# Small fp32 matmuls split over tiles of 64 or 32 columns, and a later place for two operand sets and the FFN's weight buffers

## The chip, the cores and the metric

The program runs on one core of a Trainium2 chip. The metric is the device time of one execution in microseconds (us), as the median of several executions. TensorE has two clock levels, 1.2 and 2.4 GHz; the profile prints the granted clock as a share of the higher one.

## The reference

One inference step of a decoder layer: 512 new tokens of one prompt and one token each of 8 samples share the weights, so there are 520 token columns of 2048 channels. The part that matters here:

```
h = rms_norm(x, norm1); proj = h @ w_in                 # 2048 x 9232
DeltaNet, 8 heads of 128: conv, silu, l2norm(q), l2norm(k), chunks of 64 tokens (prompt)
    one token of a sample:  S' = S*exp(g); v' = (v - k.S')*beta; S'' = S' + k v'; o = q.S''
S5, 64 groups of 16 channels and 64 complex states: a scan along the tokens, y = Re(C x)
m = sigmoid(gate_d) * (o @ w_br_dn) + sigmoid(gate_s) * (glu(y) @ w_br_s5)
x = x + m @ w_out
h = rms_norm(x, norm2)
x = x + (silu(h @ w_ffn_gate) * (h @ w_ffn_up)) @ w_ffn_down   # hidden 5632
y = rms_norm(x, norm_f)
```

## The kernel before

**Large products.** Every fp32 weight matrix is read in blocks of 8 x 128 x 128 (`raw`), split by ScalarE (`whi`) and VectorE (`wlo`) into a rounded and a remainder part, and multiplied in three passes of fp32r with 260 moving columns (L94). From the FFN on the product is a Strassen scheme (L1367): seven products per pair of two blocks, on sums and differences of weight quarters (`s`, `sm`, `se`) and on seven prepared operand sets, B11, B21, T1, T2, T3, T4 and B22, each itself split into two parts in an SBUF slot (`put`).

**Small fp32 matmuls.** These have plain fp32 operands; the trace shows each as two records of a weight load and two of a matmul. Four places matter. In each of eight S5 batches `tables(bt)` makes `pkd` (a 128 x 32 stationary operand, 128 moving columns, eight matmuls in four column blocks of one PSUM tile, then one ScalarE copy `kd` and sixteen DMAs into the table `T_`), and `outputs(bt)` makes `py` from `T_` and the tokens and from `WR` and the scanned states `X` (16 matmuls with a 128 x 128 stationary operand and 72 moving columns). Each DeltaNet head makes `pss`, the sums of squares of its keys and queries (8 matmuls, 1 moving column), after GpSimd has squared them into `sq`. The sample states make `psk`, one matmul per sample and head (64 matmuls, 2 moving columns). Another S5 product, `pb` at L634, stands on 64-column tiles already before the change: its matmuls alternate between columns 0 to 63 and 64 to 127 of the array.

**Order.** The program is written as generators that yield between parts; a scheduler places instructions on each engine's queue by their dependencies and priorities, and the queues run in that order. The S5 batches, the heads and the sample states stand among the matmuls of large products, so that TensorE has work while they wait.

**The step into the FFN.** `add_squares` sums the squares of the residual rows into `ssq`; `rstd` sums over partitions with five small matmuls (`pr`), and GpSimd and VectorE make `rt` and `ms` from it, which `rows` spreads over all partitions with matmuls against the identity (`prb`). T4 and B22 are split in 16 parts by ScalarE and VectorE before the first FFN stream begins. The gate's first four `raw` blocks are SyncE DMAs at L1410. In the Strassen scheme the product z needs block A12 and the product "11" needs A11; T2 and T1 need the sum of A21 and A22, which GpSimd makes (L1346).

Of the kernel before, what the change touches and what calls it, by code (L numbers as in the profile page):

```python
# [33 lines left out]
def hybrid_step_kernel(  # L34
# [37 lines left out]
    def weights(src, k0, nk, col):  # L72
        raw = wp.tile([P, 8, P], F32, tag="raw", name="raw", bufs=3)
        hi = wp.tile([P, 8, P], F32R, tag="whi", name="whi")
        lo = wp.tile([P, 8, P], F32R, tag="wlo", name="wlo")
        nc.sync.dma_start(
# [434 lines left out]
    def s5_steps(upp):  # L511

        with ExitStack() as es:
# [31 lines left out]
            def tables(bt):  # L545
# [130 lines left out]
            def outputs(bt):  # L676
# [59 lines left out]
    def decode(dec, dd, de, ohi, olo):  # L736
# [82 lines left out]
    def dn_steps(ohi, olo):  # L819


        with ExitStack() as es:
# [83 lines left out]
            def prep(h):  # L906
# [299 lines left out]
    def squares(pool, at=None):  # L1206
# [11 lines left out]
        def rstd(pr=None, by=None):  # L1218

            if pr is None:  # L1220
                pr = pmt("pr")
            for c in range(4):
                PE.matmul(pr[:, c:c + 1], ssq[:, c * P:(c + 1) * P], ones[:, 0:1], start=True, stop=True)
            PE.matmul(pr[0:NB, 4:5], ssq[:, NTOK:T], ones[:, 0:1], start=True, stop=True)
# [27 lines left out]
    def put(name, q, src, scale=None):  # L1252

        hi, lo = parts(XS[name], q)
        if scale is None:
            A.activation(hi, src, AF.Copy)
# [7 lines left out]
    with tc.tile_pool(name="mp", bufs=8) as mp, tc.tile_pool(name="mq", bufs=2) as mq:  # L1264
        add_squares, rstd = squares(mq)
# [59 lines left out]
        rt, ms = rstd()  # L1325
# [82 lines left out]
    def block(src, k0, nk, col):  # L1408
        raw = wq.tile([P, 8, P], F32, tag="raw", name="raw", bufs=7)
# [8 lines left out]
    wp_s.close()  # L1418
    ww = ctx.enter_context(tc.tile_pool(name="ww", bufs=5, side="right"))
# [3 lines left out]
    wq_s = ctx.enter_context(ExitStack())  # L1423
    wq = wq_s.enter_context(tc.tile_pool(name="wq", bufs=4, side="right"))
# [6 lines left out]
    XS["T4"] = slot("xT4")  # L1431
    for q in range(8):
        b = acc(q)
        put("T4", q, b[:, 0:HF])
    b22 = [fp.tile([P, 4, HF], F32, tag="hu", name="b22") for _ in range(2)]
    for j in range(2):
        A.activation(b22[j], acc_[0][:, 4 * j:4 * j + 4, HF:T], AF.Copy)
    XS["B22"] = slot("xB22")
    for q in range(8):
        put("B22", q, b22[q // 4][:, q % 4])  # L1440
    sgate = [None]
    first = [True]

    def rows(dst, v):
        prb = [pmt("prb0"), pmt("prb1")]
        for c in range(4):
            PE.matmul(prb[0][:, c * P:(c + 1) * P], v[:, c:c + 1].to_broadcast([P, P]), ident, start=True, stop=True)
# [315 lines left out]
```

## Time and profile before

| | us |
|---|---|
| median of 3 executions | 2973.57 (2972.07 to 2979.77) |
| the profiled execution | 2972.03, span 2970.3 |
| mean granted clock of TensorE | 0.98 of full speed |
| 0 to 100 | norm, first projections |
| 100 to 430 | eight S5 batches among projections |
| 430 to 1050 | eight DeltaNet heads among projections |
| 1095 to 1230 | sample states among the products of w_glu |
| 1230 to 1570 | products of w_br and w_out |
| 1570 to 1610 | step into the FFN |
| 1610 to 2480, 2480 to 2960 | FFN gate and up, FFN down |

The stages are read from the lines at which TensorE works; all times in the rows count from the span's start. A row of the timeline that shows x2 for a small fp32 matmul is one instruction, because each has two records.

### The profile page before, as it was taken

To read this page: it belongs to the slowest core of one execution; us is meant where nothing else is said; L and a number is where in the kernel's file an instruction comes from. 1 tells how busy PE (TensorE), PEld (TensorE's weight loads), DVE (VectorE), ACT (ScalarE), POOL (GpSimd) and SP (SyncE) were. 2 spreads that over 40 slices of the span, in tenths; PEclk is the share of its full clock that TensorE was granted. 3 is DMA by queue.
4 is the path that set the end of the run, shared out by engine and by line. 5 is a ranking of instruction groups with operands and counts; after the bars stand their busy time and mean duration, and the time that the engine had idled before them with its cause. 6 is when DMAs were issued, how large, how long until landed. Compare 5 with 4: busy or idle time off the path is not lost.

```text
span 2970.3 us, 60986 instructions
## 1 busy us (share of the span) xinstructions
PE 2879.3 (97%) x23869; PEld 2844.5 (96%) x23869; DVE 2055.2 (69%) x3406; ACT 1279.2 (43%) x2229; POOL 1137.2 (38%) x1656
## 2 busy tenths in 40 slices
PE   8999999999999999999998999999999999999997
PEld 7999999889999999999998999999999998999997
DVE  5766444444455334643467999999999988999997
ACT  5244333223333222222254555555555555455555
POOL 0673402554444300310143555545555543222233
PEclk9999999999999998999998999999999999999999
DMA  6444443322333354844444555555555448755542
GB/s 165 109 126 124 126 129 100 79 70 71 78 79 77 100 145 142 247 143 118 125 126 128 154 158 167 162 173 167 159 160 168 154 151 303 250 196 181 182 135 87
DMA packets 640806, 424.23 MB, mean 143 GB/s; under 512 B 66550, under 2 KB 589783, under 8 KB 636887
## 3 DMA queue, kind: packets, MB, share of 16 engines
q1 hardware_dynamic: 640518, 420.34, 47.8%
q8 instruction: 188, 3.08, 0.4%
q14 instruction: 100, 0.81, 0.1%
HBM read 342.85 MB, written 75.18 MB: 141 GB/s over the span
## 4 chain that ended last, share of the span: by engine, by line
PE 77%; POOL 9%; DVE 6%; DMA 4%; issue 3%; ACT 1%; SPq 1%; POOLq 0%; ACTq 0%; DVEq 0%
PE pt L94 30%; PE px L1367 23%; PE py L1367 12%; PE pz L1367 6%; POOL tm L963 3%; POOL uu L965 2%; DVE wlo L70 2%; DMA dx<-xdsc 2%; PE psk L768 1%; PE pss L914 1%; DVE ac L1639 1%; POOL et L604 1%; POOL et L605 0%; DVE sm L1356 0%; PE pkq L944 0%
## 5 line engine op out<-in xcount | busy, mean ns | idle before, releaser
L70 DVE TENSOR_TENSOR wlo<-raw,whi 128x512 fp32r<-128x512 f32 (+1 forms) x485 | 527.0, 1101 | 244.7 <-ACT whi L78 194.4
L78 ACT ACTIVATE whi<-raw 128x1024 fp32r<-128x1024 f32 x218 | 231.0, 1060 | 638.6 <-PE pt L94 587.6
L94 PE MATMUL pt<-hhi,wlo 128*128 128x260 f32 (+1 forms) x2336 | 493.4, 289 | 4.1 <-DVE wlo L70 4.1
L94 PE MATMUL pt<-hlo,whi 128*128 128x260 f32 (+1 forms) x2336 | 493.6, 289 | 0.0
L94 PE MATMUL pt<-hhi,whi 128*128 128x260 f32 (+1 forms) x2336 | 490.9, 289 | 1.4 <-ACT pre L876 1.3
L94 PEld LDWEIGHTS pt<-hhi,wlo 128*128 128x128 f32 x2336 | 369.9, 192 | 7.2 <-DVE wlo L70 5.0
L94 PEld LDWEIGHTS pt<-hhi,whi 128*128 128x128 f32 x2336 | 368.5, 192 | 4.0 <-ACT pre L876 1.8
L94 PEld LDWEIGHTS pt<-hlo,whi 128*128 128x128 f32 x2336 | 370.4, 191 | 1.6 <-issue 0.2
L70 DVE TENSOR_TENSOR wlo<-s,whi 128x512 fp32r<-128x512 f32 (+1 forms) x272 | 319.5, 1188 | 3.8 <-ACT whi L1362 0.7
L1346 POOL TENSOR_TENSOR s<-raw 128x1024 f32<-128x1024 f32 (+1 forms) x90 | 216.9, 2411 | 255.1 <-DVE wlo L70 126.4
L1367 PE MATMUL px<-xT,whi 128*128 128x260 f32 x1408 | 257.6, 283 | 1.1 <-ACT u L1514 1.1
L1362 ACT ACTIVATE whi<-s 128x512 fp32r<-128x512 f32 (+1 forms) x272 | 167.8, 620 | 182.3 <-PE px L1367 100.3
L1362 ACT ACTIVATE whi<-raw 128x512 fp32r<-128x512 f32 (+1 forms) x267 | 166.4, 630 | 130.3 <-PE px L1367 71.0
L1367 PEld LDWEIGHTS px<-xT,whi 128*128 128x128 f32 x1408 | 217.3, 188 | 1.3 <-ACT u L1514 1.3
L1367 PE MATMUL px<-xT,wlo 128*128 128x260 f32 x704 | 199.2, 283 | 0.0
L1367 PE MATMUL px<-wx,whi 128*128 128x260 f32 x832 | 155.2, 284 | 3.4 <-ACT whi L1362 1.5
L1346 POOL TENSOR_TENSOR s<-raws 128x512 f32<-128x512 f32 (+1 forms) x64 | 79.7, 1248 | 193.5 <-DVE wlo L70 192.2
L1367 PE MATMUL pz<-xB,whi 128*128 128x260 f32 x704 | 133.2, 287 | 2.3 <-ACT whi L1362 2.3
L1367 PEld LDWEIGHTS px<-xT,wlo 128*128 128x128 f32 x704 | 132.5, 188 | 0.0
L1367 PEld LDWEIGHTS px<-wx,whi 128*128 128x128 f32 x832 | 127.5, 189 | 5.2 <-ACT whi L1362 2.1
L1367 PE MATMUL px<-xB,whi 128*128 128x260 f32 x704 | 129.5, 284 | 0.2 <-ACT whi L1362 0.2
L1367 PE MATMUL px<-xt,whi 128*128 128x260 f32 x704 | 129.3, 284 | 0.0
(586 smaller groups left out, 7611.6 us busy)
## 6 DMA issues: line engine op xcount, KB each, us to landing
raw<-in_w_in_dram SPq DMA_DIRECT2D x146, 512.0 KB
raw<-in_w_ffn_gate_dram SPq DMA_DIRECT2D x88, 512.0 KB
raw<-in_w_ffn_up_dram SPq DMA_DIRECT2D x88, 512.0 KB
xT<-hx SPq DMA_DIRECT2D x88, 260.0 KB
raws<-in_w_ffn_down_dram SPq DMA_DIRECT2D x44, 512.0 KB
xB<-hx SPq DMA_DIRECT2D x66, 260.0 KB
raw<-in_w_out_dram SPq DMA_DIRECT2D x32, 512.0 KB
hs<-xT SPq DMA_DIRECT2D x12, 1040.0 KB
```

The source lines that it names most:

```text
L70: V.tensor_tensor(out, full, hi.bitcast(F32), ALU.subtract)
L78: A.activation(hi[:, :nk], raw[:, :nk], AF.Copy)
L94: PE.matmul(pt[:, h, 0:c1 - c0], w_[:, j], x[:, c0:c1], start=k == 0 and i == 0, stop=k == n - 1 and i == 2)
L604: G.tensor_tensor(t1[:, r, :, 0:n], E[:, r, :, 0:n], rr, ALU.mult)
L768: PE.matmul(psk[:, 2 * i:2 * i + 2], sts[b][:, h], kqn[:, :, i], start=True, stop=True)
L914: PE.matmul(pss[:, s * 4 + c:s * 4 + c + 1], sq[:, s, c * P:(c + 1) * P], ones[:, 0:1], start=True, stop=True)
L963: G.tensor_tensor(tm[:, :, 0:31 - j], uu[:, :, j:j + 1].to_broadcast(sh), dx[:, j, j + 1:32].unsqueeze(1).to_broadcast(sh), ALU.mult)
L965: G.tensor_tensor(uu[:, :, j + 1:32], uu[:, :, j + 1:32], tm[:, :, 0:31 - j], ALU.add)
L1346: G.tensor_tensor(t, a, b, op)
L1362: A.activation(hi, w_in_, AF.Copy)
L1367: PE.matmul(o, w_[:, q - q0], x_, start=start and q == 0 and i == 0, stop=q == kp - 1 and i == 2, skip_group_check=not start)
L1639: V.tensor_tensor(a[:, j], o, a[:, j], ALU.add)
```

## The change

Six edits. `pkd` writes its four blocks to four column groups of 32 (positions 0, 32, 64, 96 of the array) with the two passes outermost, and `kd` is copied by four instructions of 32 x 128. `py`, `psk` and `pss` split each stationary operand of 128 columns into two of 64, on column groups 0 and 64: 128 to 256 matmuls for `py`, 64 to 128 each for `psk` and `pss`. `rstd` runs inside the first FFN stream, between its products, with `rows` after the third and fifth. T4 and B22 are split in four groups, behind products three to six, and pinned in that order. The FFN's `raw` blocks get a pool of their own (7 buffers) in the space that the projections' weights leave; A12 is loaded ahead of A11. In the FFN's down part all weight blocks come from that pool, and ten instead of eight halves of the operands lie in slots, four instead of six in the pool `hs`.

```diff
+                for r in range(2):
+                    for g in range(GB):
+                        PE.matmul(pkd[g * 32:(g + 1) * 32, 0:P], bd[:, r, g].rearrange("p a c -> p (a c)"),
+                                  W[:, r, g, 0:8].rearrange("p d c -> p (d c)"), start=r == 0, stop=r == 1,
+                                  tile_position=(0, g * 32))
+                kd = s1.tile([32, GB, P], F32, name="kd")
                 for g in range(GB):
-                    for r in range(2):
-                        PE.matmul(pkd[0:32, g * P:(g + 1) * P], bd[:, r, g].rearrange("p a c -> p (a c)"),
-                                  W[:, r, g, 0:8].rearrange("p d c -> p (d c)"), start=r == 0, stop=r == 1)
-                kd = s1.tile([32, GB, P], F32, name="kd")
-                A.activation(kd, pkd[0:32].rearrange("p (g m) -> p g m", g=GB), AF.Copy)
+                    A.activation(kd[:, g], pkd[g * 32:(g + 1) * 32, 0:P], AF.Copy)
...
+                        ms_ = [slice(m, m + 64) for m in range(0, P, 64)]
                         o = py[:, g * 72:(g + 1) * 72]
-                        PE.matmul(o, T_[:, g * 2 + g2], U_[:, g * 2 + g2, 0:72], start=True, stop=False)
-                        PE.matmul(o, WR[:, g, g2], X[:, g, g2, 0:72], start=False, stop=True)
+                        for m in ms_:
+                            PE.matmul(o[m], T_[:, g * 2 + g2, m], U_[:, g * 2 + g2, 0:72], start=True, stop=False)
+                        for m in ms_:
+                            PE.matmul(o[m], WR[:, g, g2, m], X[:, g, g2, 0:72], start=False, stop=True)
...
-                PE.matmul(psk[:, 2 * i:2 * i + 2], sts[b][:, h], kqn[:, :, i], start=True, stop=True)
+                for m in range(0, P, 64):
+                    PE.matmul(psk[m:m + 64, 2 * i:2 * i + 2], sts[b][:, h, m:m + 64], kqn[:, :, i],
+                              start=True, stop=True)
...
-                        PE.matmul(pss[:, s * 4 + c:s * 4 + c + 1], sq[:, s, c * P:(c + 1) * P], ones[:, 0:1],
-                                  start=True, stop=True)
+                        for m in range(0, P, 64):
+                            PE.matmul(pss[m:m + 64, s * 4 + c:s * 4 + c + 1], sq[:, s, c * P + m:c * P + m + 64],
+                                      ones[:, 0:1], start=True, stop=True)
...
-        rt, ms = rstd()
...
+    wq = ctx.enter_context(tc.tile_pool(name="wq", bufs=7, side="right"))
...
-        A_ = [[block(src, 8 * j, 8, (2 * i + n) * P) for j in range(2)] for n in range(2)]
+        A_ = [[block(src, 8 * j, 8, (2 * i + n) * P) for j in (1, 0)][::-1] for n in range(2)]
...
-            rows(rstd2, rt)
-            todo.append(lambda: rows(rms2, ms))
+            v = rstd(pinned=True)
+            rt.append(v[0])
+            sets = last_sets()
+            todo.extend([lambda: (rows(rstd2, v[0], "e"), sets[0]()), sets[1],
+                         lambda: (rows(rms2, v[1], "m"), sets[2]()), sets[3]])
...
-            hs_.append(ctx.enter_context(tc.tile_pool(name="hs", bufs=6)))
+            hs_.append(ctx.enter_context(tc.tile_pool(name="hs", bufs=4)))
...
-            if i < 8:
+            if i < 10:
                 return wx[i // 2][:, i % 2 * HW:(i % 2 + 1) * HW].rearrange("p (a b c) -> p a b c", a=4, b=2)
...
-                if first:
-                    raw = wq.tile([P, 8, P], F32, tag="raw", name="raw", bufs=7)[:, 0:2 * kp]
-                else:
-                    r = nth("raw", 6 if hs_ else 4)
-                    if r < 4:
-                        raw = raw_c[:, r * 1024:r * 1024 + 2 * kp * P].rearrange("p (k m) -> p k m", m=P)
-                    else:
-                        raw = hs_[1].tile([P, 8, P], F32, tag="rawx", name="rawx", bufs=2)[:, 0:2 * kp]
+                raw = wq.tile([P, 8, P], F32, name="raw")[:, 0:2 * kp]
```

The new function `last_sets` returns the four groups: four `put` of T4 and one ScalarE copy of a half of B22's source in each of the first two, four `put` of B22 in each of the others.

Three places of the order. First TensorE's queue at the sample states, before (L768 is `psk`, L94 the products of w_glu around it):

```order
L94 MATMUL pt<-g5hi,wlo 128x260 x2
L768 MATMUL psk<-kqn,st 128x2 x4
L94 MATMUL pt<-g5hi,whi 128x260 x2
L94 MATMUL pt<-g5lo,whi 128x260 x2
L768 MATMUL psk<-kqn,st 128x2 x2
...
L768 MATMUL psk<-kqn,st 128x2 x26
...
L768 MATMUL psk<-kqn,st 128x2 x32
```

And after (L774 is `psk`):

```order
L94 MATMUL pt<-g5hi,wlo 128x260 x2
L774 MATMUL psk<-kqn,st 64x2 x5
L94 MATMUL pt<-g5hi,whi 128x260 x2
L94 MATMUL pt<-g5lo,whi 128x260 x2
L774 MATMUL psk<-kqn,st 64x2 x3
...
L774 MATMUL psk<-kqn,st 64x2 x56
...
L774 MATMUL psk<-kqn,st 64x2 x64
```

The four runs of `psk` stay where they were, with the same matmuls of the large products between them; each has about twice the instructions, on operands half as wide.

Second TensorE's queue at the end of w_out (L94) and the begin of the first FFN stream, before (`pr` is `rstd`'s sum, `prb` is `rows`, `pz` and `px` are the products z and "11"):

```order
L94 MATMUL pt<-mhi,wlo 128x260 x2
L1223 MATMUL pr<-ones,ssq 128x1 x4
L1224 MATMUL pr<-ones,ssq 8x1
L1447 MATMUL prb_18549<-ident,rt 128x128 x4
L1448 MATMUL prb_18550<-ident,rt 128x8
L1367 MATMUL pz<-xB_17259,whi 128x260 x2
```

And after (L1375 is the Strassen product, `rstd_14990` the tile that now holds the sums of squares; between the first z row and `pr` stand the rest of z and of "11"):

```order
L94 MATMUL pt<-mhi,wlo 128x260 x2
L1375 MATMUL pz<-xB_17538,whi 128x260 x2
...
L1375 MATMUL px<-xB_17537,wlo 128x260
L1232 MATMUL pr<-ones,rstd_14990 128x1 x4
L1233 MATMUL pr<-ones,rstd_14990 8x1
L1375 MATMUL px<-xT_17539,whi 128x260 x2
```

The products z and "11" follow w_out's last matmul at once; `pr` stands behind them, `prb` later still.

Third SyncE's queue of DMAs at the same place, before (`asc` is the store of a residual row):

```order
L1302 DMA asc_14724<-acc_14703 128x520
L1302 DMA asc_14725<-acc_14703 128x520
L1302 DMA asc_14726<-acc_14703 128x520
L1410 DMA raw<-in_w_ffn_gate_dram 128x8x128 x4
L1410 DMA raw<-in_w_ffn_up_dram 128x8x128 x4
```

And after:

```order
L1311 DMA asc_15004<-acc_14983 128x520
L1311 DMA asc_15005<-acc_14983 128x520
L1418 DMA raw<-in_w_ffn_gate_dram 128x8x128 x2
L1311 DMA asc_15006<-acc_14983 128x520
L1418 DMA raw<-in_w_ffn_gate_dram 128x8x128 x2
L1418 DMA raw<-in_w_ffn_up_dram 128x8x128 x4
```

The gate's first two blocks, now A12 and A11, stand ahead of the last store. The first of them waits for w_out's last matmul (its buffer's former reader); before, it waited for `pr` and for VectorE's last split of w_out's rows.

## Rows read from the trace of the kernel before

**Rows 1.** The page, part 4: the chain that ended last, shares by engine.

```profile
PE 77%; POOL 9%; DVE 6%; DMA 4%; issue 3%; ACT 1%; SPq 1%; POOLq 0%; ACTq 0%; DVEq 0%
```

**Rows 2.** Stretches: length, busy us (xcount) of PE, PEld, DVE, ACT, POOL; PEclk, DMA share, GB/s.

```profile
100.00:227.00 127.00, 124.52 (x1101) 121.80 (x1099) 83.37 (x201) 49.36 (x72) 98.29 (x268) 1.00 0.46 117
227.00:430.00 203.00, 200.91 (x1780) 197.86 (x1781) 106.62 (x221) 79.90 (x112) 66.79 (x189) 1.00 0.48 128
1155.00:1190.00 35.00, 35.00 (x223) 35.00 (x222) 15.76 (x23) 5.37 (x8) 0.00 (x0) 0.71 0.18 58
1230.00:1570.00 340.00, 340.00 (x2843) 340.00 (x2842) 170.52 (x183) 109.70 (x156) 61.06 (x60) 1.00 0.45 132
1610.00:2310.00 700.00, 699.85 (x5828) 699.50 (x5828) 644.25 (x881) 382.22 (x726) 371.04 (x258) 1.00 0.53 161
```

**Rows 3.** Timeline, PE, first S5 batch: start us, us, line, operation, xcount.

```profile
127.07 1.93 PE L583 MATMUL pkd<-W,bd 128*32 128x128 f32 x16
...
128.93 1.22 PE L634 MATMUL pb<-uz,QT 128*64 128x72 f32 x32
...
130.08 0.51 PE L94 MATMUL pt<-hhi,wlo 128*128 128x260 f32 x2
...
130.43 0.40 PE L94 MATMUL pt<-hhi,whi 128*128 128x260 f32 x2
```

**Rows 4.** Timeline, PE, `py` of the fourth S5 batch, first and last L688 row.

```profile
259.39 0.44 PE L688 MATMUL py<-X,WR 128*128 128x72 f32 x2 [0.97 <-DVE X L665]
...
261.90 0.28 PE L688 MATMUL py<-X,WR 128*128 128x72 f32 x1
```

**Rows 5.** Waits of PE in 227 to 430: us in total, times, longest.

```profile
PE py L688 <- DVE X L665: 1.0, 1, 1.0
```

**Rows 6.** Timeline, PE, `pss` of one head.

```profile
797.23 0.38 PE L914 MATMUL pss<-ones,sq 128*128 128x1 f32 x2 [1.96 <-POOL sq L910]
...
798.00 1.70 PE L914 MATMUL pss<-ones,sq 128*128 128x1 f32 x14
799.56 0.78 PE L933 MATMUL pgc<-triu,gg 128*128 128x128 f32 x2
```

**Rows 7.** Timeline, PE, the two long runs of `psk` and what follows each.

```profile
1155.01 8.53 PE L768 MATMUL psk<-kqn,st 128*128 128x2 f32 x52
1163.40 0.78 PE L94 MATMUL pt<-g5hi,whi 128*128 128x260 f32 x2
...
1171.31 10.39 PE L768 MATMUL psk<-kqn,st 128*128 128x2 f32 x64
1181.57 0.78 PE L94 MATMUL pt<-g5hi,whi 128*128 128x260 f32 x2
...
1189.02 0.33 PE L783 MATMUL pq<-qk,ones 128*128 128x64 f32 x2
```

**Rows 8.** Timeline, 1570 to 1600: PE, then DVE, POOL and SyncE's queue.

```profile
1573.15 1.05 PE L1223 MATMUL pr<-ones,ssq 128*128 128x1 f32 x8 [2.75 <-DVE ssq L1216]
...
1576.44 2.07 PE L1447 MATMUL prb<-ident,rt 128*128 128x128 f32 x8 [2.11 <-POOL rt L117]
...
1581.33 0.80 PE L1367 MATMUL pz<-xB,whi 128*128 128x260 f32 x2 [2.29 <-ACT whi L1362]
...
1591.86 1.13 PE L1447 MATMUL prb<-ident,ms 128*128 128x128 f32 x8 [1.23 <-DVE se L1356]
...
1593.28 0.51 PE L1367 MATMUL py<-xT,whi 128*128 128x260 f32 x2
...
1579.64 2.46 DVE L70 TENSOR_TENSOR xB<-b,xB 128x260 fp32r<-128x260 f32 x7
...
1584.50 4.70 POOL L1346 TENSOR_TENSOR s<-raw 128x1024 f32<-128x1024 f32 x2 [8.11 <-DMA raw<-in_w_ffn_gate_dram]
...
1574.64 3.79 SPq L1410 DMA_DIRECT2D raw<-in_w_ffn_gate_dram  x4
```

**Rows 9.** DMA view, 1574 to 1590: rate in 40 slices of 0.4 us.

```profile
GB/s 0 0 0 0 79 159 301 315 343 342 314 297 293 251 262 294 292 321 315 302 294 288 291 292 291 291 289 289 292 292 289 288 293 288 289 234 99 6 0 0
```

More of the change, by code (lines that the diff above doesn't have):

```diff
@@ L1216, in add, with rstd @@
                 (V if t >= KD - 2 else G).tensor_tensor(ssq[:, h], ssq[:, h], sqt[:, h], ALU.add)
-        def rstd(pr=None, by=None):
+        def rstd(pr=None, by=None, pinned=False):
             if pr is None:
                 pr = pmt("pr")
+            pin = tc.keep_in_program_order if pinned else lambda m: m
             for c in range(4):
-                PE.matmul(pr[:, c:c + 1], ssq[:, c * P:(c + 1) * P], ones[:, 0:1], start=True, stop=True)
-            PE.matmul(pr[0:NB, 4:5], ssq[:, NTOK:T], ones[:, 0:1], start=True, stop=True)
+                pin(PE.matmul(pr[:, c:c + 1], ssq[:, c * P:(c + 1) * P], ones[:, 0:1], start=True, stop=True))
+            pin(PE.matmul(pr[0:NB, 4:5], ssq[:, NTOK:T], ones[:, 0:1], start=True, stop=True))
             rt, ms = (cp.tile([P, 5], F32, name=n) for n in (("rt", "ms") if by is None else ("rtf", "msf")))
@@ L1422, in hybrid_step_kernel @@
     rms2 = sp.tile([P, T], F32, name="rms2", bufs=1)
-    wq_s = ctx.enter_context(ExitStack())
-    wq = wq_s.enter_context(tc.tile_pool(name="wq", bufs=4, side="right"))
     def wparts(n):
@@ L1430, in hybrid_step_kernel, with last_sets, t4, b22_ @@
     fp = fp_s.enter_context(tc.tile_pool(name="fp", bufs=2))
[L1431 to L1441, printed above, removed]
-    first = [True]
-    def rows(dst, v):
-        prb = [pmt("prb0"), pmt("prb1")]
+    sgate, rt = [None], []
+    first = [True]
+    def last_sets():
+        pin = tc.keep_in_program_order
+        b22 = []
+        def t4(q0):
+            if not q0:
+                XS["T4"] = slot("xT4")
+            for q in range(q0, q0 + 4):
+                put("T4", q, acc(q)[:, 0:HF], pin=pin)
+            b22.append(fp.tile([P, 4, HF], F32, tag="hu", name="b22"))
+            pin(A.activation(b22[-1], acc_[0][:, q0:q0 + 4, HF:T], AF.Copy))
+        def b22_(q0):
+            if not q0:
+                XS["B22"] = slot("xB22")
+            for q in range(q0, q0 + 4):
+                put("B22", q, b22[q0 // 4][:, q - q0], pin=pin)
+        return [lambda: t4(0), lambda: t4(4), lambda: b22_(0), lambda: b22_(4)]
+    def rows(dst, v, tag):
+        prb = [pmt("prb0", tag), pmt("prb1", tag)]
+        pin = tc.keep_in_program_order
         for c in range(4):
-            PE.matmul(prb[0][:, c * P:(c + 1) * P], v[:, c:c + 1].to_broadcast([P, P]), ident, start=True, stop=True)
-        PE.matmul(prb[1][:, 0:NB], v[0:NB, 4:5].to_broadcast([NB, P]), ident[0:NB, 0:NB], start=True, stop=True)
+            pin(PE.matmul(prb[0][:, c * P:(c + 1) * P], v[:, c:c + 1].to_broadcast([P, P]), ident,
+                          start=True, stop=True))
+        pin(PE.matmul(prb[1][:, 0:NB], v[0:NB, 4:5].to_broadcast([NB, P]), ident[0:NB, 0:NB], start=True, stop=True))
         V.tensor_copy(dst[:, 0:NTOK], prb[0])
@@ L1574, in hybrid_step_kernel @@
         acs = [flat(slot("ac0").bitcast(F32))]
-        raw_c = flat(slot("raws").bitcast(F32))
+        wx4 = flat(slot("wx4"))
         acs.append(flat(slot("ac1").bitcast(F32)))
-        wx.append(flat(x3.tile([P, 8, T], F32R, tag="x3", name="wx3")))
+        wx.extend([flat(x3.tile([P, 8, T], F32R, tag="x3", name="wx3")), wx4])
         accs = [quad(acs[i // 4][:, i % 4 * 4 * HF:(i % 4 + 1) * 4 * HF]) for i in range(8)]
-        turn_ = {"raw": 0, "h": 0}
-        def nth(kind, n):
-            i = turn_[kind]
-            turn_[kind] = (i + 1) % n
-            return i
+        turn_ = [0]
         def half():
-            i = nth("h", 14)
-            if i < 8:
+            i = turn_[0]
+            turn_[0] = (i + 1) % 14
+            if i < 10:
                 return wx[i // 2][:, i % 2 * HW:(i % 2 + 1) * HW].rearrange("p (a b c) -> p a b c", a=4, b=2)
@@ L1604, in load_acc, with load_w @@
                 nc.sync.dma_start(flat(accs[i][:, 2 * n:2 * n + 2]), asc[2 * i + n])
-        def load_w(q0, kp, i, first=False):
+        def load_w(q0, kp, i):
             A_ = []
             for n in range(2):
-                if first:
-                    raw = wq.tile([P, 8, P], F32, tag="raw", name="raw", bufs=7)[:, 0:2 * kp]
-                else:
-                    r = nth("raw", 6 if hs_ else 4)
-                    if r < 4:
-                        raw = raw_c[:, r * 1024:r * 1024 + 2 * kp * P].rearrange("p (k m) -> p k m", m=P)
-                    else:
-                        raw = hs_[1].tile([P, 8, P], F32, tag="rawx", name="rawx", bufs=2)[:, 0:2 * kp]
+                raw = wq.tile([P, 8, P], F32, name="raw")[:, 0:2 * kp]
                 nc.sync.dma_start(raw, w_ffn_down[2 * q0 * P:2 * (q0 + kp) * P, (2 * i + n) * P:(2 * i + n + 1) * P]
@@ L1700, in streams @@
             q0 = 0
-            A_ = load_w(0, CHUNKS[0], 0, True)
+            A_ = load_w(0, CHUNKS[0], 0)
             nxt = load_x(0)
```

14 lines of the change are left out of this document (7 added, 7 removed).

## The prediction

> **What bounds the kernel now.** I read the chain that ended last first. TensorE carries 77% of it, GpSimd and VectorE 15% together [rows 1]: a change pays if it shortens TensorE's queue, or a wait that stands in it. The stretches say where that holds [rows 2]. From 227 to 430, the later S5 batches, TensorE is busy 200.9 of 203.0 us. From 100 to 227 it is as busy, but GpSimd works 98.3 of 127 us in a serial chain (the tables), and the scanned states come so late that TensorE waits for them; time saved there I expect to return as a wait. From 1155 to 1190 the granted clock is 0.71: the sample states. From 1610 on TensorE never waits, with VectorE busy 644 of 700 us. Then I read the timeline at the four small products and the step into the FFN.
>
> **Halves of 64 columns.** What a split costs or saves is read from `pb`, which stands in the same form already. Its 16 instructions (x32) start at 128.93 and the large product resumes at 130.08 [rows 3]: 1.15 us, 0.072 each. An unsplit one of 128 columns costs 0.223: seven `pss` from 798.00 to 799.56 [rows 6]. `py` agrees: 11 instructions from 259.39 to 261.90 [rows 4], 0.228 each. So two halves cost 0.144 where one whole costs 0.223, a saving of 0.079 for each old instruction. The 0.072 contains the drain at the run's end. Around the run the price of changing tiles stays: the L94 pair after it takes 0.35 (130.08 to 130.43) [rows 3] where two large matmuls take 0.24 (340 us for 2843) [rows 2], so 0.11, and about as much at the entry: 0.2 for each run. The order after shows 46 such runs in place of 9, so 37 times 0.2, 7.4 us, is to be paid out of the savings below; with the drain inside a run counted too, about 0.35 each.
>
> The Trainium skill, "TensorEngine Tiling (Array Packing)", section "Key Properties", says that a change of tiling mode drains TensorE. It speaks against this change, and rows 3 agree, with 0.11 us at the exit. Charged at 0.35 for each of 37, that rule alone would take 13 us and leave about half of the gain.
>
> **py.** Per batch 32 x 0.072 + 0.2 = 2.5 us for 16 x 0.223 = 3.57: 1.07 less.
>
> **pkd.** Eight instructions from 127.07 to 128.93, 1.86 us [rows 3]. On four column groups two can overlap as in `pb` (0.93 left) or all four (0.47). That bounds the gain at 0.93 and 1.4; I take 1.2. The three additional ScalarE copies `kd` lie beside TensorE's other work (ScalarE is busy 79.9 of 203 us [rows 2]); behind them only the table's DMAs wait, and the first `py` half waits for these.
>
> **S5 together.** Five of the eight batches lie behind 227: 5 x 2.27 = 11.4. One of them waits for X already, 1.0 us [rows 5], and returns its `py` gain there. I take 10. Bounds: 3, if most of the batches run into X; 16, if the three batches before 227 gain two thirds as well.
>
> **pss.** Per head 8 x 0.079 = 0.63 saved, less about two switches of 0.2, since its first instruction stands apart [rows 6]: 0.23, eight heads 1.8 us. It stands right behind the wait for `sq` (1.96), so it is on the heads' own chain. Bounds: a gain of 3.4, or a loss of 2 with each switch at 0.35.
>
> **psk.** The two long runs hold 58 instructions, and 48 large matmuls stand behind each. At full clock that is 58 x 0.223 + 96 x 0.12 = 24.5 us; the rows give 34.0, from 1155.01 to 1189.02 [rows 7]. The clock costs the other 9.5: it falls within each run and is restored only well into the large matmuls (0.71 in this stretch [rows 2]). After: 120 x 0.072 + 96 x 0.12 + 0.4 = 20.6 at full clock. A run is 4.2 us instead of 8.4 and 10.3 (1155.01 to 1163.40, 1171.31 to 1181.57). I take half of the clock's cost, 4.7, as left: 25.3, a gain of 8.7, and 0.3 at the two short runs: 9. Bounds: nothing lost to the clock gives 13.4; all of it and dearer switches, 4.
>
> The Trainium skill, "TensorE: Matmul & The Clock Gate", section "LDWEIGHTS (loading the stationary operand)", gives a weight load a time in proportion to its columns (128 columns by that figure an estimated 107 ns, 64 columns 53). With two records an instruction that is 0.213 and 0.107 us: the whole one agrees with 0.223, the half one lies above the 0.072 of rows 3. If loads alone counted, one after the other, two halves would cost what one whole costs, and the splits would pay nothing.
>
> **The step into the FFN.** TensorE waits four times [rows 8]: 2.75 for `ssq`, 2.11 for `rt`, 2.29 for the first split weights, 1.23 in front of the second `prb`; 8.4 together. After, z and "11" follow w_out directly, and `pr` and `prb` come where their inputs are long done. What is late next is A12. Its DMA can issue at 1570.4 (w_out's end: 1573.15 less 2.75) instead of 1574.64. Data flow at 290 GB/s, 1.8 us for a block, and a first block takes 3.1 us for its bytes to have moved [rows 9] and at most 4.4 (GpSimd's start on the fourth at 1584.50, less three blocks). So it lands near 1574.4, and with 0.6 of splitting z starts near 1575.2 instead of 1581.33: 6.1 less, of which `pr` and both `prb` (1.05, 2.07, 1.13) are not saved but moved, and only the first two stood in front of z. The fourth block, which T2 and T1 need through GpSimd, comes 4.2 us earlier less 0.9 for the `asc` store now in between (260 KB at the same rate): 3.3. Between these I take 5. Bounds: 0, if the 16 splits of VectorE (seven took 2.46 [rows 8], so 5.6 in all) delay the weights of products three to six in a stage where it has 8% to spare; 13, if the half-speed clock of the idle stretch goes too.
>
> **FFN down.** The same 14 operand halves and seven weight blocks instead of six; loads leave earlier. Costed at nothing, since VectorE's splitting, which the change leaves as it is, keeps TensorE's queue fed there as it does from 1610 to 2310 [rows 2]. If that cover fails, a block that comes late costs at most its 1.8 us [rows 9], and two such make the bound of 4 either way.
>
> **Sum.** 10 + 1.8 + 9 + 5 = 25.8 off the profiled execution's 2972.03 (a span of 2970.3 and 1.7 around it, which the change leaves) gives 2946.2. The median is 1.5 above that execution, so I say 2948.
>
> **Rivals.**
> Spent again (0.14): S5 gains run into X and into the tables' DMAs (only 3 us left), `pss` nothing, `psk` 4, the step 3: 10 us, 2963. For it: GpSimd's share before 227 and the wait in rows 5. Against: 227 to 430 has that one wait only.
> More than that (0.16): the shorter runs of `psk` keep the clock up (13.4), the first three batches gain too (16), the step loses its slow stretch (10), `pss` 3: 43 us, 2930. For it: the clock's cost is in the rows; against: a run of 4 us is still long enough for the fall that came within the 8.4.
> No change (0.08): VectorE's 16 splits return the step's gain, and the small products wait on X, `sq` and the state loads: 2972.
> Slower (0.06): the halves do not overlap when they share one moving operand, in contrast to `pb`, whose two halves have different ones. A pair then takes 0.288 instead of 0.144; the point from which it decides is 0.223. `py` loses 5.2 in five batches, `psk` 4.4 and 4.4 more at low clock, `pss` 4.2, and 37 switches 7.4; the step gives 5 back: about 20, 2994. That is also where the page on weight loads points. Against it: nothing in rows 3 ties the overlap to the operand.
>
> **How the numbers follow.** My forecast has 0.56, its own range 2939 to 2956. The range to hold the time 8 times in 10 takes in the two cases on its sides, most of each: 2927 to 2963. 0.3% is 9 us, about what a measurement of this kernel can tell from no change. The forecast and the first two rivals lie beyond it on the faster side: 0.86; same 0.08; slower 0.06.
>
> **What would show it.** In the changed profile: `py` rows of a batch within 2.5 us and `pkd` within 1; the wait for X in more than one batch if the gains are spent; the stretch from `psk`'s third run to its `pq` near 25 us with a granted clock above 0.8; the first z row within 5 us of w_out's last row, and no wait for `rt` in front of it; VectorE's splits of T4 between those of weights without a new wait of TensorE. I am wrong if 64-column pairs take more than 0.2, or if a wait for `wlo` in the first three FFN streams grows by more than 5 us.

## The result and the profile after

The changed kernel takes 2944.52 us (median of four executions, 2943.89 to 2948.4) against 2976.32 for the kernel before beside it: a ratio of 0.9898, interval 0.988 to 0.9916. It is faster by 1.0%, near the forecast of 2948 and inside its range. A later repetition gave 2944.28 (2943.06 to 2946.04) against 2974.72, ratio 0.9895, interval 0.988 to 0.9909.

The total came out well; its terms did not all. To see them, take the large matmuls (260 moving columns): every trace of this study has 21456 of them, in the same stages, so the time from the start of one number to the start of another is the time of a stage, with what the small products and the waits cost in it. These are worked out from the traces, in us: the S5 batches up to the 1300th (about 235 us) and from there to the 2700th, the heads to the 6500th, the sample states to the 7800th, the step into the FFN from the 10200th to the 11100th, and the end of the up products with the begin of the down part from the 17400th to the 18400th.

```
                       S5 early  S5 late   heads   sample   step    down
                       600-1300  -2700     -6500   -7800    10200-  17400-
before                   115.09   207.61   621.76   191.73   131.26  133.66
ffn_only                 115.15   208.72   625.44   194.35   130.11  131.46
pss_whole                112.81   200.90   623.52   181.23   129.66  132.98
changed                  112.70   200.16   621.99   180.92   130.37  131.28
changed_again            112.68   200.83   617.27   179.93   131.17  129.32
small_only               113.05   200.67   620.93   179.59   128.63  133.62
psk_grouped              112.71   199.66   619.60   191.09   130.19  131.20
pkd_pass_inner           113.59   201.70   617.62   183.61   127.74  131.44
psk_spread               112.64   200.66   617.02   201.40   131.25  131.72
psk_quarters             112.52   199.98   618.27   181.77   132.29  131.95
sets_later               112.74   201.79   616.25   178.45   128.19  131.53
quarters_sets_later      112.36   198.59   619.09   180.05   127.93  129.11
```

The rows other than `before` and `changed` are the experiments below. One program's stage scatters from execution to execution: the heads of `before` and `ffn_only` are the same program and differ by 3.7 us, those of `changed` and `changed_again` by 4.7. So the single pair `before` and `changed` would say that the split of `pss` gave nothing; means over the kernels that share a stage's program say otherwise. By them: S5 early -2.3 and late -7.7 (two kernels with whole products, ten with split ones), heads -4.9 (three with `pss` whole, nine split), sample states -12.4 (two whole, and six with the order of the changed kernel), the step +0.4 (two with the old step, eight with the new), down -2.4 (two and ten; TensorE waits 8.8 and 8.2 us there with the old buffers, 6.0 to 7.1 with the new). Unrounded they sum to -29.4; the medians say -31.8 and -30.4.

The changed kernel, stretches: length, busy us (xcount) of the five engines, granted clock, DMA share, GB/s. Compare [rows 2].

```profile
100.00:227.00 127.00, 120.92 (x1205) 115.13 (x1204) 85.31 (x201) 51.44 (x85) 97.20 (x267) 1.00 0.45 112
227.00:430.00 203.00, 199.59 (x2017) 194.60 (x2017) 107.27 (x224) 84.88 (x129) 69.90 (x193) 1.00 0.53 138
1145.00:1165.00 20.00, 20.00 (x301) 19.83 (x299) 14.19 (x17) 3.76 (x6) 0.00 (x0) 0.74 0.31 96
```

Up to 227 us TensorE now idles 6 of 127 us where it idled 2.5, with GpSimd busy as before: most of what the three early batches saved turned into waits. From 227 on it idles 3.4 us, little more than before.

The small products in the changed kernel's timeline of TensorE, to be read beside [rows 3] and [rows 4] (L636 is the old L634):

```profile
126.79 0.64 PE L583 MATMUL pkd<-W,bd 128*32 128x128 f32 x16
127.36 1.22 PE L636 MATMUL pb<-uz,QT 128*64 128x72 f32 x32
...
258.36 0.35 PE L693 MATMUL py<-X,WR 128*64 128x72 f32 x4 [0.90 <-DVE X L667]
258.53 0.29 PE L691 MATMUL py<-uz,s5m 128*64 128x72 f32 x4
...
260.04 0.30 PE L693 MATMUL py<-X,WR 128*64 128x72 f32 x4
```

A row of x4 is now a pair of halves, one old instruction. `pkd` takes 0.57 us (126.79 to 127.36) instead of 1.86. From 258.53 to 260.04 stand 24 halves: 0.063 us each.

The sample states, beside [rows 7]:

```profile
1144.52 3.77 PE L774 MATMUL psk<-kqn,st 128*64 128x2 f32 x112
1148.22 0.80 PE L94 MATMUL pt<-g5hi,whi 128*128 128x260 f32 x2
...
1156.84 3.90 PE L774 MATMUL psk<-kqn,st 128*64 128x2 f32 x128
1160.67 0.51 PE L94 MATMUL pt<-g5hi,whi 128*128 128x260 f32 x2
...
1168.05 0.33 PE L790 MATMUL pq<-qk,ones 128*128 128x64 f32 x2
```

The two runs take 3.70 and 3.83 us instead of 8.39 and 10.26, and the stretch to `pq` 23.5 instead of 34.0. The clock still falls (0.74 in the window above), for a shorter time. Which level a run meets differs from execution to execution: in `changed_again` and in `sets_later` the first of the two runs took 3.36 us, and the granted clock was 1.00 in it and in the 2 us behind it.

The sums of squares in the first two heads, before and then after:

```profile
475.46 1.84 PE L914 MATMUL pss<-ones,sq 128*128 128x1 f32 x16
477.17 0.47 PE L933 MATMUL pgc<-triu,gg 128*128 128x128 f32 x2
...
531.96 3.57 PE L914 MATMUL pss<-ones,sq 128*128 128x1 f32 x16 [5.44 <-POOL sq L910]
535.40 0.78 PE L933 MATMUL pgc<-triu,gg 128*128 128x128 f32 x2
```

```profile
466.98 1.10 PE L922 MATMUL pss<-ones,sq 128*64 128x1 f32 x32
468.00 0.49 PE L941 MATMUL pgc<-triu,gg 128*128 128x128 f32 x2
...
522.85 1.87 PE L922 MATMUL pss<-ones,sq 128*64 128x1 f32 x32 [5.46 <-POOL sq L917]
524.65 0.80 PE L941 MATMUL pgc<-triu,gg 128*128 128x128 f32 x2
```

In the first head, at a granted clock of 1.00, the run takes 1.02 us instead of 1.71; in the second, at 0.50 in both kernels, 1.80 instead of 3.44.

The step into the FFN, beside [rows 8]: TensorE, then VectorE, GpSimd and SyncE's queue.

```profile
1554.74 0.77 PE L1375 MATMUL pz<-xB,whi 128*128 128x260 f32 x2 [5.03 <-issue]
...
1563.28 0.95 PE L1232 MATMUL pr<-ones,rstd 128*128 128x1 f32 x8
...
1567.29 0.77 PE L1375 MATMUL px<-xT,whi 128*128 128x260 f32 x2 [2.94 <-DVE rt L1237]
...
1580.98 0.58 PE L1375 MATMUL px<-xt,wlo 128*128 128x260 f32 x1 [3.80 <-DVE wlo L70]
...
1562.62 2.84 DVE L1364 TENSOR_TENSOR sm<-s,raw 128x512 f32<-128x512 f32 x1 [5.01 <-POOL s L1354]
...
1566.73 0.42 DVE L1530 TENSOR_TENSOR p<-px,p 128x260 f32<-128x260 f32 x1
...
1567.13 0.14 DVE L1237 TENSOR_SCALAR rt<-pr 8x1 f32<-8x1 f32 x1
...
1567.38 0.69 DVE L1364 TENSOR_TENSOR sm<-s,raw 128x512 f32<-128x512 f32 x1
...
1574.95 3.50 DVE L70 TENSOR_TENSOR xT<-acc,xT 128x260 fp32r<-128x260 f32 x2
...
1580.25 1.28 DVE L70 TENSOR_TENSOR wlo<-s,whi 128x512 fp32r<-128x512 f32 x2
...
1560.19 4.71 POOL L1354 TENSOR_TENSOR s<-raw 128x1024 f32<-128x1024 f32 x2 [8.34 <-DMA raw<-in_w_ffn_gate_dram]
...
1575.60 2.56 POOL L1354 TENSOR_TENSOR s<-raw 128x1024 f32<-128x1024 f32 x1
...
1549.78 1.01 SPq L1418 DMA_DIRECT2D raw<-in_w_ffn_gate_dram  x2
```

The four waits of before (8.4 us) are gone: z starts right when its first block is there, and `pr` and `prb` wait for nothing. In their place stand three others, 5.03, 2.94 and 3.80 us: for the first block's load, in front of T2 and for the remainder weights of T3. The second ends with VectorE's queue: the profile names `rt` (L1237, to 1567.27), and just ahead of it the sum that reads the tile to which T2 adds (L1530) ended at 1567.15; both stand behind `sm` and the split of its result. Which of the two released T2 the rows don't tell apart.

The kernel before has two rows of the same kind that [rows 8] does not hold, the first behind its end (TensorE, then VectorE):

```profile
1602.60 0.58 PE L1367 MATMUL pz<-xB,wlo 128*128 128x260 f32 x1 [3.02 <-DVE wlo L70]
...
1586.90 3.46 DVE L1356 TENSOR_TENSOR sm<-s,raw 128x512 f32<-128x512 f32 x2 [2.40 <-POOL s L1346]
```

With that wait of 3.02, TensorE's waits in the step's stage are 11.6 us before and 12.0 after.

### The profile page after: what moved, and what is told of

Its sections match the earlier page's. It is cut to its first block, busy times and chain, and to the rows that moved or that the text cites. A ratio compares the mean times of both kernels' runs of the same rounds, so it can differ in the third digit from the quotient of the medians.

```text
span 2946.7 us, 62042 instructions
## 1 busy us (share of the span) xinstructions
PE 2850.7 (97%) x24381; PEld 2810.7 (95%) x24381; DVE 2061.2 (70%) x3406; ACT 1283.1 (44%) x2253; POOL 1140.3 (39%) x1656
## 4 chain that ended last, share of the span: by engine, by line
PE 77%; POOL 8%; DVE 6%; DMA 5%; issue 2%; ACT 1%; SPq 1%; POOLq 0%; ACTq 0%; DVEq 0%
PE pt L94 31%; PE px L1375 23%; PE py L1375 12%; PE pz L1375 6%; DVE wlo L70 2%; POOL tm L971 2%; POOL uu L973 2%; DMA dx<-xdsc 2%; DMA raw<-in_w_in_dram 1%; DVE ac L1651 1%; POOL et L607 1%; PE pss L922 0%; POOL et L606 0%; POOL sq L917 0%; DMA x<-in_x_prompt_dram 0%
## 5 line engine op out<-in xcount | busy, mean ns | idle before, releaser
L70 DVE TENSOR_TENSOR wlo<-raw,whi 128x512 fp32r<-128x512 f32 (+2 forms) x626 | 660.5, 1067 | 248.5 <-ACT whi L78 204.8
L1354 POOL TENSOR_TENSOR s<-raw 128x1024 f32<-128x1024 f32 (+2 forms) x184 | 331.6, 1803 | 548.7 <-DVE wlo L70 345.2
L94 PE MATMUL pt<-hhi,wlo 128*128 128x260 f32 (+1 forms) x2336 | 492.1, 289 | 4.5 <-DVE wlo L70 4.4
L94 PE MATMUL pt<-hhi,whi 128*128 128x260 f32 (+1 forms) x2336 | 493.4, 289 | 2.4 <-ACT pre L883 1.7
L94 PE MATMUL pt<-hlo,whi 128*128 128x260 f32 (+1 forms) x2336 | 494.4, 289 | 0.0
L94 PEld LDWEIGHTS pt<-hhi,wlo 128*128 128x128 f32 x2336 | 369.6, 191 | 8.3 <-DVE wlo L70 6.0
L94 PEld LDWEIGHTS pt<-hhi,whi 128*128 128x128 f32 x2336 | 369.0, 191 | 6.1 <-ACT pre L883 2.9
L94 PEld LDWEIGHTS pt<-hlo,whi 128*128 128x128 f32 x2336 | 370.9, 191 | 2.2 <-issue 0.4
L1370 ACT ACTIVATE whi<-raw 128x512 fp32r<-128x512 f32 (+1 forms) x408 | 250.1, 617 | 213.7 <-PE px L1375 123.6
L70 DVE TENSOR_TENSOR wlo<-s,whi 128x512 fp32r<-128x512 f32 (+1 forms) x272 | 325.5, 1210 | 4.0 <-ACT whi L1370 1.3
L1375 PE MATMUL px<-xT,whi 128*128 128x260 f32 x1408 | 259.3, 284 | 4.0 <-DVE rt L1237 2.9
L1375 PEld LDWEIGHTS px<-xT,whi 128*128 128x128 f32 x1408 | 218.5, 189 | 4.3 <-issue 3.0
L1375 PE MATMUL px<-xT,wlo 128*128 128x260 f32 x704 | 199.6, 284 | 0.0
L1375 PE MATMUL px<-wx,whi 128*128 128x260 f32 x1024 | 190.2, 283 | 2.5 <-DVE ac L1651 2.0
L1375 PEld LDWEIGHTS px<-wx,whi 128*128 128x128 f32 x1024 | 157.0, 188 | 3.5 <-DVE ac L1651 1.8
L1375 PE MATMUL px<-wx,wlo 128*128 128x260 f32 x512 | 142.2, 283 | 1.1 <-DVE wlo L70 1.1
L1375 PE MATMUL pz<-xB,whi 128*128 128x260 f32 x704 | 132.0, 285 | 5.0 <-issue 5.0
L1375 PEld LDWEIGHTS px<-xT,wlo 128*128 128x128 f32 x704 | 133.2, 189 | 0.0
L1375 PE MATMUL px<-xB,whi 128*128 128x260 f32 x704 | 129.7, 284 | 0.0
L1375 PE MATMUL py<-xT,whi 128*128 128x260 f32 x704 | 129.0, 283 | 0.2 <-DVE hg L1548 0.2
```

The costliest lines, as they stand in the source:

```text
L70: V.tensor_tensor(out, full, hi.bitcast(F32), ALU.subtract)
L94: PE.matmul(pt[:, h, 0:c1 - c0], w_[:, j], x[:, c0:c1], start=k == 0 and i == 0, stop=k == n - 1 and i == 2)
L1354: G.tensor_tensor(t, a, b, op)
L1370: A.activation(hi, w_in_, AF.Copy)
L1375: PE.matmul(o, w_[:, q - q0], x_, start=start and q == 0 and i == 0, stop=q == kp - 1 and i == 2, skip_group_check=not start)
```

## The experiments

Each is told as an edit of the kernel before or of the changed kernel. Ratios are against the kernel before.

**The small products alone.** The kernel before with the four split products, nothing of the FFN's edits.

> The kernel before with the four small products alone on narrow tiles, the step into the FFN and its buffers as before. Theory 1 (the parts add): the S5 stage gives 10 us and psk 11, pss nothing, so 21 us less than before, about 2952, and the large products from w_br on run 20 to 21 us earlier than before in the two traces. Theory 2 (the FFN edits carry the gain, and the small products only fill waits): under 10 us less, above 2963.

2946.04 us, ratio 0.991 (0.9891 to 0.9929), 28 us less than before. The stages S5, heads and sample states are those of the changed kernel, within their scatter. The gain is more than the 21 us of theory 1, which took the sample states and the heads too small. Theory 2 falls: these four products alone bring nearly all of the changed kernel's 30 to 32 us.

**The FFN's edits alone.** The changed kernel with the four products whole.

```diff
-                        for m in range(0, P, 64):
-                            PE.matmul(pss[m:m + 64, s * 4 + c:s * 4 + c + 1], sq[:, s, c * P + m:c * P + m + 64],
-                                      ones[:, 0:1], start=True, stop=True)
+                        PE.matmul(pss[:, s * 4 + c:s * 4 + c + 1], sq[:, s, c * P:(c + 1) * P], ones[:, 0:1],
+                                  start=True, stop=True)
...
```

> The changed kernel with the four small products whole again: only the step into the FFN, its buffers and the order of the operand sets differ from before. Theory 1: the step gives about 1 us and the down part about 2, so 3 us less than before, 2971, within what a measurement can tell. Theory 2 (the step's earlier start is worth its 5 us and the down part 2): 7 us less, 2967. In the trace z starts 5 to 6 us earlier against w_out's end in both; theory 1 wants waits for VectorE of about 3 and 4 us in the next products, theory 2 wants none.

2972.37 us over ten executions, ratio 0.9997 (0.9985 to 1.0009): no difference that can be measured. By the stages the step gives 1.1, less than it scatters, and the down part 2.2. TensorE's waits in front of T2 and T3 are 2.73 and 3.77 us. Theory 1 stands.

**pss whole.** The part of the edit above that is shown, in the changed kernel.

> The changed kernel with pss alone whole again. Theory 1 (splitting pss gains nothing: the switches and longer stretches at the low clock around the wait for sq take what the pairs save): no difference to the changed kernel beyond 2 us, 2943 to 2947, and the half-speed stretches around pss are shorter by about 3 us in most heads. Theory 2 (the split saves 0.2 us a head as forecast): 2 us slower than the changed kernel. Theory 3 (the split itself lowers the clock for longer): 4 us or more faster, under 2941.

2950.73 us (2947.75 to 2952.82), ratio 0.9921 (0.9902 to 0.994), against 2944.5 and 2944.3 of the changed kernel: some 6 us slower. Theories 1 and 3 fall; theory 2 has the direction and is too small. The shorter half-speed stretches that theory 1 wanted did not come: 51 us between 425 and 1040, where the changed kernel has 61 and 44 in its two traces.

**Halves that do not alternate.** In the changed kernel, the same 128 half matmuls of `psk` in another order.

```diff
-        for b in range(NB):
-            for h in range(HEADS):
-                i = h * 8 + b
-                for m in range(0, P, 64):
...
+        for b0 in range(0, NB, 4):
+            for m in range(0, P, 64):
+                for b in range(b0, b0 + 4):
+                    for h in range(HEADS):
+                        i = h * 8 + b
```

> The changed kernel with the halves of psk in another order: all halves on columns 0 to 63 of four samples first, then all on columns 64 to 127, same instructions and same count. Theory 1 (a pair overlaps only when its two halves stand next to each other on different column groups): an instruction costs about 0.12 us instead of 0.06, the two long runs take 7 us each at full clock and more at the lower one, 8 to 12 us slower than the changed kernel, so psk loses most of its gain. Theory 2 (a half costs half by its width alone): no difference, about 2945.

2955.73 us, ratio 0.9945 (0.9925 to 0.9966), 11 us slower than the changed kernel. Its timeline of TensorE:

```profile
1142.24 7.73 PE L775 MATMUL psk<-kqn,st 128*64 128x2 f32 x116
1149.90 0.80 PE L94 MATMUL pt<-g5hi,whi 128*128 128x260 f32 x2
...
1157.87 10.62 PE L775 MATMUL psk<-kqn,st 128*64 128x2 f32 x128
1168.42 0.80 PE L94 MATMUL pt<-g5hi,whi 128*128 128x260 f32 x2
```

58 halves take 7.66 us, 0.132 each, where 56 alternating ones took 3.70. Part of that is the clock: the granted clock is 0.85 in the first run and 0.66 in the second, against 0.89 and 1.00 in the changed kernel and 0.67 in both runs before. Put to full clock (length times granted clock, over the count), a half on one group costs an estimated 0.11 us, an alternating one 0.06 and a whole one before 0.216. So two halves on one group cost what one whole costs, and the stage is as long as before (191.1 against 191.7). Theory 1 holds.

**The order of pkd's passes.** In the changed kernel, blocks outermost and the two passes innermost, on the same four column groups.

```diff
-                for r in range(2):
-                    for g in range(GB):
+                for g in range(GB):
+                    for r in range(2):
```

> The changed kernel with the two passes of pkd innermost again, still on four column groups: each block's two matmuls follow each other on the same group. Theory 1 (neighbours on different column groups overlap, on the same group they do not): the run of eight takes about 1 us in place of 0.57, 0.5 us more in each of eight batches, 2 to 3 us later at the end of the S5 stage. Theory 2 (four groups run side by side whatever the order): 0.57 us again, no difference.

Two executions, 2946.56 us, ratio 0.9906 (0.9878 to 0.9933). The run is nearly as short as in the changed kernel:

```profile
128.25 0.67 PE L583 MATMUL pkd<-W,bd 128*32 128x128 f32 x16
128.85 1.22 PE L636 MATMUL pb<-uz,QT 128*64 128x72 f32 x32
```

0.60 us against 0.57. Two neighbours on the same group do not hold up the next group; the run of 58 on one group in `psk_grouped` did, and lengths between were not tried. Theory 2 holds.

**The operand sets later.** In the changed kernel:

```diff
-            todo.extend([lambda: (rows(rstd2, v[0], "e"), sets[0]()), sets[1],
-                         lambda: (rows(rms2, v[1], "m"), sets[2]()), sets[3]])
+            todo.extend([lambda: rows(rstd2, v[0], "e"), lambda: None,
+                         lambda: (rows(rms2, v[1], "m"), sets[0]()), sets[1],
+                         lambda: (sets[2](), sets[3]())])
```

> The changed kernel with the splits of T4 and B22 placed later: those of T4 behind the product T3 and behind z of the second stream, those of B22 behind that stream's product 11; the same instructions otherwise. Theory 1 (the step into the FFN gave back its gain because VectorE's splits of T4 stand ahead of the split weights of T1 and T3): the 3.8 us wait in front of T3's remainder weights falls under 1 us, the large products from the second stream on run 2 to 4 us earlier than in the changed kernel, about 2942. Theory 2 (the wait is for GpSimd's sums of weight quarters, whatever VectorE does): the wait stays, no difference. Theory 3 (later splits come too late for the products that read them): a new wait in front of T4 or B22, 2 us or more slower.

2940.85 us (2939.92 to 2947.21), ratio 0.9891 (0.9871 to 0.9911); not to be told from the changed kernel by the time. The stage takes 128.2, and 127.9 in the combination below, against a mean of 130.4 for the eight kernels without this edit; but those eight reach from 127.7 (`pkd_pass_inner`) to 132.3, so a gain of 2 us is likely and not shown. Its waits of TensorE from 1540 to 1600 (us in total, times, longest):

```profile
PE pz L1375 <- issue: 5.0, 1, 5.0
PE px L1375 <- DVE rt L1237: 3.5, 1, 3.5
PE px L1375 <- DVE wlo L70: 1.7, 2, 0.9
PE py L1375 <- DVE hg L1548: 0.4, 1, 0.4
```

The wait of 3.80 in front of T3 is gone; two of 0.8 to 0.9 and one of 0.4 stand in the streams behind. Theory 1 holds for that wait; its 2 to 4 us of time are not shown. The other two waits stay, 5.0 and 3.5.

**psk in runs of one sample.** In the changed kernel, a yield after each sample.

```diff
-            if b % 4 == 3:
-                yield
+            yield
```

> The changed kernel with a yield after each sample of psk instead of after four, so that its 128 matmuls stand in runs of at most 16 among 48 large matmuls each. Theory 1 (what psk still loses to the clock comes from the length of a run): no stretch at the low clock in the sample states' products, 5 us saved there, about 2 us of it spent on six more switches of tiles and on later sums: 2 to 4 us faster, 2941. Theory 2 (any run of small products lowers the clock): no gain, or 1 to 2 us slower by the switches.

2965.33 us, ratio 0.9968 (0.9957 to 0.998), 21 us slower than the changed kernel, for a reason that neither theory had. A stretch over the runs, and a row of TensorE's timeline later:

```profile
1143.00:1177.00 34.00, 34.00 (x377) 32.96 (x376) 17.05 (x18) 8.65 (x11) 0.00 (x0) 1.00 0.49 145
```

```profile
1245.53 0.77 PE L94 MATMUL pt<-ohi,whi 128*128 128x260 f32 x2 [15.43 <-DVE gd L1286]
```

The clock stays at 1.00, as theory 1 said: behind none of the runs of 16 halves, 1.0 us, does it fall. But six more yields put all that follows `psk` six places later among the large products; the sample states end late, and the next stage waits 15.4 us for its gates.

**psk in runs of two samples.** The same number of yields as in the changed kernel: two instead of four at the state loads, four instead of two at `psk`.

```diff
             nc.sync.dma_start(st, state_dn_ssm[0, b].rearrange("h k v -> k h v"))
-            if b % 2:
+            if b % 4 == 3:
                 yield
...
-            if b % 4 == 3:
+            if b % 2:
                 yield
```

> The changed kernel with psk in runs of two samples, 32 half matmuls each, 48 large ones apart; the state loads are issued in two groups instead of four, so that the last run keeps its place in the queue and nothing behind it comes later. Theory 1 (the length of a run lowers the clock, and spreading by sample was slow only because everything behind psk moved back by six places): no low-clock stretch within the sample states' products, no new wait behind, 4 to 5 us faster than the changed kernel by the trace, about 2940. Theory 2 (spreading costs by itself): as slow as the spread by sample, above 2955.

2948.86 us (2939.23 to 2952.99), ratio 0.9905 (0.9884 to 0.9926): no gain. No new wait stands behind, so theory 2 falls; but theory 1 falls too. The timeline at the end of the second of the four runs (its last ten records, then large matmuls):

```profile
1138.82 0.44 PE L774 MATMUL psk<-kqn,st 128*64 128x2 f32 x10
1139.18 0.68 PE L94 MATMUL pt<-g5hi,whi 128*128 128x260 f32 x2
1139.66 0.64 PE L94 MATMUL pt<-g5lo,whi 128*128 128x260 f32 x2
1140.09 0.64 PE L94 MATMUL pt<-g5hi,wlo 128*128 128x260 f32 x2
```

The pairs of large matmuls behind the run start 0.43 us apart instead of 0.24: the low level, after a run of only 2.0 us. It comes behind two of the three full runs, and again behind two of three in the combination below; behind the run of 3.36 us of `changed_again` it did not come. So the length of a run alone does not settle it; what does is left open.

**Both together.**

> The changed kernel with psk in runs of 32 half matmuls and the splits of T4 and B22 placed later, both edits together. If they add: 4 to 5 us from the clock and 2 us from the step into the FFN, 2937 to 2939, about 36 us under the kernel before. If the FFN takes the time back: 2940 to 2942.

2942.79 us (2939.47 to 2944.27), ratio 0.9888 (0.9873 to 0.9903). The step's stage is again 2 us under the mean, the clock's 4 to 5 us are not there; with `sets_later` the fastest version of this study, ahead of the changed kernel by no more than the measurement's uncertainty.

**The changed kernel again,** as the reference of the last two.

> The changed kernel as it is, on the same chip as the two above, as their reference: 2943 to 2948. In its trace the half-speed stretches around pss move from those of the first profile by several us, if what differs in the heads between two executions is the clock and not the program.

2944.28 us. Its heads are 4.7 us shorter than in the first profile, with 44 instead of 61 us at the lower clock level between 425 and 1040 (summed from the traces' clock records). Over the twelve traces the heads take 0.29 us more for each us at the lower level (a line fitted to them, with a step of its own for `pss` whole), so the 17 us at that level account for the 4.7. The difference between two executions of one program is as large as a whole term of the forecast.

## Why the prediction was right, and where it was not

The mechanism was right where the gain lies, in the small products. That the total fits as well as it does is partly luck: `psk`, `pss` and the down part gave about 3, 2 to 3 and 2 us more than forecast, and the step 5 less.

**Halves of 64 columns: right.** Forecast 0.072 us each, measured 0.063; the rest of the 0.072 is the end of `pb`'s run, counted in. The whole one is also a little cheaper than the 0.223 read from [rows 6], where the clock falls just before the end: 1.71 us for eight in the first head above, 0.214 each. The terms charge only 4.6 of the 7.4 us that the forecast names for switches. The rival that the halves do not overlap when they share a moving operand is refuted: `py`, `pss` and `psk` all share it. `psk_grouped` shows that the overlap carries the gain. There the 0.11 for a half at full clock agrees with the 0.107 estimated from the Trainium skill, "TensorE: Matmul & The Clock Gate", section "LDWEIGHTS (loading the stationary operand)": on one column group the halves do go one after the other, and the rule's consequence, no gain from the split, is what that kernel shows. On alternating groups it does not apply.

**S5: right in the sum (10 against 10.0), not in its places.** The 1.2 for `pkd` measured 1.29 (1.86 to 0.57). The late batches gave 7.7 instead of 10: TensorE's waits there grew from 1.3 to 3.4 us, 0.6 of it for X, now in two batches and not one, and 1.4 for split weights of the large products, which the forecast did not name. The early ones gave 2.3 instead of nothing.

**pss: mis-sized, 1.8 against 3.7 to 4.9,** with an upper bound of 3.4. Two terms failed. The charge of two switches a head (0.2 each) was too high: where the run is in two pieces at full clock, they take 0.24 and 1.48 us whole (`pss_whole`, sixth head) and 0.21 and 1.02 split (`changed_again`, sixth head), 0.49 less and not 0.23. And all eight heads were priced at full clock: the second, at a granted clock of 0.50 in both kernels, saves 1.64 where the first saves 0.69. How sure the size is: the three stages with `pss` whole span 3.7 us, the nine split ones 5.7, and the whole ones had 4 us more at the lower level on average; at equal time there the fitted line of `changed_again` gives 3.7 instead of 4.9. So 3 to 6 is as near as it goes. Part of what the heads gain returns in front of `sq`: TensorE waits there 24.5 us in the changed kernel's seven later heads and 21.6 before.

**psk: mis-sized, 9 against 12.4.** The runs were shorter than forecast (3.8 instead of 4.2) and the share of the clock's cost that stays is under the half that was assumed: 23.5 us to `pq` instead of 25.3, a gain of 10.5. The granted clock in that stretch is 0.78, not above 0.8 as the forecast said. The rest of the 12.4 lies outside the stretch that the forecast looked at, or in the scatter of the stage (178.5 to 183.6 among the six).

**The step into the FFN: wrong, 5 against nothing.** The first half came as said: z starts 5.9 us earlier against the 10200th large matmul (1554.74, where 1581.33 less the 20.7 of that place would be 1560.6), and no wait for `ssq` or `rt` is left in front of it. GpSimd's first sum, which needs the fourth block, starts 3.6 us earlier by the same measure, for the forecast's 3.3. The failed step is that a lead between these two, and with it the removed waits of 8.4 us, would reach the end of the stream. The lead is 2.6 us at the 10440th large matmul and 0.9 from the 10512th on, and the stage's waits are 12.0 us, where they were 11.6.

T2 could not start before the sums, so the lead beyond 3.6 turned into a wait of 2.94 in front of it, in place of 1.23 in front of the second `prb`; and `pr` and the first `prb` now take 1.1 and 1.4 us behind z, which the forecast called moved and did not take off its 6.1. On this chain VectorE's subtraction `sm` took 2.84 us; the next one of the same shape took 0.69. It ended at 1565.46, just behind GpSimd's two sums (1560.19 to 1564.90): in these rows VectorE stands while GpSimd adds. It was as slow before (3.46 for two), so it is part of what T2 waits for and not a new loss. The Trainium skill, "SBUF — State Buffer", section "SBUF: two separate sides", states that a VectorE operation with two SBUF inputs and a GpSimd operation that reads SBUF lock each other out, whichever starts first, for a whole instruction; these rows agree.

In front of T3 two of the moved T4 splits took 3.50 us (seven splits of that size took 2.46 before [rows 8]), across GpSimd's sum for the second stream (1575.60 to 1578.16), and the remainder weights of T3 stood behind them. That wait of 3.80 stands where the kernel before had 3.02 in front of the second stream's z, behind its own slow `sm`, a wait that the forecast did not list. It is the bound of nothing gained that the forecast gave, by its own mechanism; `sets_later` removes it, with 2 us likely gained. That GpSimd's sums slow `sm` was not tried by an experiment; it rests on the rows.

**FFN down: 0 forecast, 2.4 gained,** inside the bound of 4. `ffn_only` has it (131.5), `small_only` has not (133.6, and 133.7 before), so it belongs to the FFN's edits, by their place to its buffers; which of them was not tried apart.

**The rivals.** "Spent again" happened in the step and in the early batches only. "More than that" had the right sign for the sample states and for `pss`.

## What to carry to other kernels

A small fp32 matmul whose stationary operand fills 128 columns can be split into halves on two column groups, or quarters on four, for some 0.6 or 0.3 of its time, if the halves alternate. A stage's price should come from several executions: one pair of profiles would have put one term at nothing. And a split or sum that is moved in order to fill an engine's idle time should be checked against what the engine's neighbour does then: VectorE work moved beside GpSimd's sums took several times its length.

## What the runs showed of the hardware that was not expected

Four column groups of 32 run side by side whether neighbours in the queue share a group or not (0.57 and 0.60 us for eight matmuls, 1.86 on one group), while a long run of 64-column halves on one group costs an estimated 0.11 for each at full clock against 0.06 in alternation. With 48 large matmuls between them, runs of 2.0 us of two-column matmuls were followed by a stretch at the lower clock level in four of six cases, runs of 1.0 us (16 halves) in none of six. Executions of one program differ by 17 us in the time spent at that level around the heads (44 and 61), and the heads' stage by 4.7. A VectorE operation of 0.7 us took 2.84 where it met GpSimd's sum, before and after the change alike.
